# A batched fp32 matmul with 1 MiB loads and stores: a small early DMA from an input into the output, and stores six batches behind the loads

## Chip, cores, metric

One core of one Trainium2 chip. The metric is the device time of one execution in microseconds (us), lower is better. The profile's span is about 2.0 us shorter than this time (125.2 against 127.17 us).

## The reference

```
a: (16, 512, 512) float32      # batch, k, m
b: (16, 512, 512) float32      # batch, k, n
out = np.matmul(a.transpose(0, 2, 1), b)      # (16, 512, 512) float32
```

Each batch reads 2 MiB and writes 1 MiB: 50.33 MB in all.

## The kernel before

One queue, SyncE's, issues all loads and stores, 1 MiB each: 128 partitions with 8192 contiguous bytes each. VectorE casts a and b to bf16, TensorE multiplies, ScalarE copies PSUM to an output tile. The store of batch i comes in the queue behind the load of batch i + LAG.

```python
LAG = 4
NL = LAG + 1          # load buffers
NB = 2                # bf16 buffers
NO = LAG + 2          # output buffers
...
def load(i):
    j = i % NL
    if i >= NL:
        nc.sync.wait_ge(s_acast, i - NL + 2)
    nc.sync.dma_start(a_ts[j][:], a_v[i]).then_inc(s_a[j], 16)
    nc.sync.dma_start(b_ts[j][:], b_v[i]).then_inc(s_b[j], 16)

def store(i):
    nc.sync.wait_ge(s_ev1, i + 1)
    nc.sync.dma_start(out_v[i], o_ts[i % NO][:]).then_inc(s_o[i % NO], 16)

for i in range(LAG):
    load(i)
for i in range(batch):
    if i + LAG < batch:
        load(i + LAG)
    store(i)
for j in range(NO):
    nc.sync.wait_ge(s_o[j], 16 * len(range(j, batch, NO)))
...                   # VectorE casts, TensorE matmuls (16 of 128x512 per batch)
for i in range(batch):
    if i >= NO:
        nc.scalar.wait_ge(s_o[i % NO], 16 * (i // NO))
    for h in range(H):
        nc.scalar.wait_ge(s_mm, H * i + h + 1)
        nc.scalar.copy(
            out=o_ts[i % NO][:, 2 * h:2 * h + 2, :], in_=ps_ts[(i % NB) * H + h][:]
        ).then_inc(s_ev1 if h else s_ev0, 1)
```

Of the kernel before, what the change touches and what calls it, by code (L numbers as in the profile page):

```python
# [1 line left out]

# [4 lines left out]

@with_exitstack
def kernel(
    ctx: ExitStack,  # L10
    tc: tile.TileContext,
    a: bass.AP,
    b: bass.AP,
    out: bass.AP,
):
    nc = tc.nc
    P = 128
    batch, K, M = a.shape
    _, _, N = b.shape
    KO = K // P  # L20
    MO = M // P
    f32 = mybir.dt.float32
    bf = mybir.dt.bfloat16



    a_v = a.rearrange("bat (ki ko) m -> bat ki ko m", ko=KO)
    b_v = b.rearrange("bat (ki ko) n -> bat ki ko n", ko=KO)
    out_v = out.rearrange("bat (mi mo) n -> bat mi mo n", mo=MO)

    LAG = 4
    NL = LAG + 1
    NB = 2
    NO = LAG + 2
    H = MO // 2

    pool = ctx.enter_context(tc.tile_pool(name="sb", bufs=1))
    psum = ctx.enter_context(tc.tile_pool(name="ps", bufs=1, space=bass.MemoryType.PSUM))
    a_ts = [pool.tile([P, KO, M], f32, name=f"a{j}") for j in range(NL)]
    b_ts = [pool.tile([P, KO, N], f32, name=f"b{j}") for j in range(NL)]  # L40
    abf_ts = [pool.tile([P, KO, M], bf, name=f"abf{j}") for j in range(NB)]
    bbf_ts = [pool.tile([P, KO, N], bf, name=f"bbf{j}") for j in range(NB)]
    o_ts = [pool.tile([P, MO, N], f32, name=f"o{j}") for j in range(NO)]
    ps_ts = [psum.tile([P, 2, N], f32, name=f"ps{j}") for j in range(NB * H)]

    s_a = [tc.alloc_semaphore(f"s_a{j}") for j in range(NL)]
    s_b = [tc.alloc_semaphore(f"s_b{j}") for j in range(NL)]
    s_o = [tc.alloc_semaphore(f"s_o{j}") for j in range(NO)]
    s_acast = tc.alloc_semaphore("s_acast")
    s_bcast = tc.alloc_semaphore("s_bcast")  # L50
    s_mm = tc.alloc_semaphore("s_mm")
    s_ev0 = tc.alloc_semaphore("s_ev0")
    s_ev1 = tc.alloc_semaphore("s_ev1")

    with tc.tile_critical(no_gpsimd_drain=True):  # L55
# [6 lines that stand above are left out]
            nc.sync.dma_start(b_ts[j][:], b_v[i]).then_inc(s_b[j], 16)  # L62

        def store(i):
            nc.sync.wait_ge(s_ev1, i + 1)
            nc.sync.dma_start(out_v[i], o_ts[i % NO][:]).then_inc(s_o[i % NO], 16)

# [10 lines that stand above are left out]
            n = 16 * (i // NL + 1)  # L78
            if i >= NB:
                nc.vector.wait_ge(s_mm, H * (i - NB + 1))  # L80
            nc.vector.wait_ge(s_a[i % NL], n)
            nc.vector.tensor_copy(out=abf_ts[i % NB][:], in_=a_ts[i % NL][:]).then_inc(s_acast, 1)  # L82
            nc.vector.wait_ge(s_b[i % NL], n)
            nc.vector.tensor_copy(out=bbf_ts[i % NB][:], in_=b_ts[i % NL][:]).then_inc(s_bcast, 1)  # L84

        nc.tensor.sem_inc(s_ev0, 1)
        with nc.tensor.Fori(0, batch // NB):
            for u in range(NB):
                a_m = abf_ts[u][:].rearrange("p ko (mi mo) -> p ko mo mi", mo=MO)
                nc.tensor.wait_ge(s_bcast, 1).then_inc(s_bcast, -1)  # L90


                nc.tensor.wait_ge(s_ev0, 1).then_inc(s_ev0, -1)  # L93
                for mo in range(MO):
                    for ko in range(KO):
                        mm = nc.tensor.matmul(  # L96
                            ps_ts[u * H + mo // 2][:, mo % 2, :],
                            a_m[:, ko, mo, :],
                            bbf_ts[u][:, ko, :],
                            start=(ko == 0),  # L100
                            stop=(ko == KO - 1),
                        )
                    if mo % 2:
                        mm.then_inc(s_mm, 1)

        for i in range(batch):
            if i >= NO:
                nc.scalar.wait_ge(s_o[i % NO], 16 * (i // NO))
# [7 lines that stand above are left out]
# [1 line left out]
_INS = ['a', 'b']  # L117
_OUTS = [((16, 512, 512), 'float32')]


# [23 lines left out]
```

## Time and profile before

| | before |
|---|---|
| time, median of 3 | 126.56 us (126.44 to 126.85) |
| the profiled execution | 127.17 us, span 125.2 us |
| DMA queue | 96.6% of 16 engines' span |
| TensorE, VectorE, ScalarE busy | 59%, 31%, 27% |

From the page: the span, the rows of the granted TensorE clock, of the DMA engines' busy share and of their rate in 40 equal slices (3.1 us each), and the line of the one DMA queue (packets, MB, share of 16 engines).

```profile
span 125.2 us, 757 instructions
...
PEclk9999999999997786999558997786999558997785
DMA  3999999999999999999999999999999999999971
GB/s 81 422 422 427 429 422 427 422 348 432 387 419 416 429 429 401 419 429 440 424 424 419 432 437 422 424 419 435 437 419 422 422 432 432 424 424 424 416 317 81
...
q1 hardware_dynamic: 6912, 50.33, 96.6%
```

The DMA engines hardly ever rest: the kernel is bound by them. Two slices stand out, 348 near 26 us, and 317 near the end.

The view by windows puts numbers on these. Its columns: stretch, its length, then busy time and instruction count of PE, PEld, DVE, ACT and POOL, the granted clock, the DMA engines' busy share, and GB/s.

```profile
core 0: us, PE busy (x) PEld busy (x) DVE busy (x) ACT busy (x) POOL busy (x), PEclk, DMA share, GB/s
14.00:26.00 12.00, 10.49 (x46) 4.96 (x45) 5.66 (x6) 5.39 (x6) 0.00 (x0) 1.00 1.02 425
26.00:28.00 2.00, 2.00 (x11) 0.91 (x9) 0.84 (x1) 1.01 (x1) 0.00 (x0) 1.00 0.99 311
...
60.00:90.00 30.00, 20.33 (x64) 7.91 (x64) 10.33 (x9) 8.11 (x8) 0.00 (x0) 0.78 1.01 427
118.00:119.00 1.00, 0.22 (x2) 0.00 (x0) 0.00 (x0) 0.74 (x1) 0.00 (x0) 1.00 0.80 336
119.00:120.00 1.00, 0.00 (x0) 0.00 (x0) 0.00 (x0) 0.27 (x1) 0.00 (x0) 1.00 0.37 156
120.00:121.00 1.00, 0.00 (x0) 0.00 (x0) 0.00 (x0) 0.00 (x0) 0.00 (x0) 1.00 0.94 393
121.00:122.00 1.00, 0.00 (x0) 0.00 (x0) 0.00 (x0) 0.00 (x0) 0.00 (x0) 0.50 1.00 410
122.00:123.00 1.00, 0.00 (x0) 0.00 (x0) 0.00 (x0) 0.00 (x0) 0.00 (x0) 0.50 0.66 270
```

From 26 to 28 us the engines are busy (0.99) and yet move 311 instead of 425 GB/s: their packets take longer. From 119 to 120 us they are not busy (0.37): they have nothing to do. The second case is the "hole".

The chain of waits (start, length, what) shows what the hole waits for: batch 15's matmuls and its last copy.

```profile
112.87 0.04 issue
112.92 5.32 PE ps L96 x16
118.24 0.02 issue
118.26 1.01 ACT o L111
```

The last store is issued when that copy is done, in the timeline (start, length, engine, instruction):

```profile
118.26 1.01 ACT L111 COPY o<-ps 128x1024 f32<-128x1024 f32 x1 [1.85 <-PE ps L96]
119.30 0.33 SPq L66 DMA_DIRECT2D out_dram<-o  x1
```

### The profile page before, as it was taken

To read this page: it belongs to the slowest core of one execution; us is meant where nothing else is said; L and a number is where in the kernel's file an instruction comes from. 1 tells how busy PE (TensorE), PEld (TensorE's weight loads), DVE (VectorE), ACT (ScalarE), POOL (GpSimd) and SP (SyncE) were. 2 spreads that over 40 slices of the span, in tenths; PEclk is the share of its full clock that TensorE was granted. 3 is DMA by queue.
4 is the path that set the end of the run, shared out by engine and by line. 5 is a ranking of instruction groups with operands and counts; after the bars stand their busy time and mean duration, and the time that the engine had idled before them with its cause. 6 is when DMAs were issued, how large, how long until landed. Compare 5 with 4: busy or idle time off the path is not lost. (4 is left out here: it accounts for less than half of the span.)

```text
span 125.2 us, 757 instructions
## 1 busy us (share of the span) xinstructions
PE 74.0 (59%) x256; PEld 30.5 (24%) x256; DVE 39.3 (31%) x32; ACT 33.7 (27%) x33; POOL 0.2 (0%) x4
## 2 busy tenths in 40 slices
PE   0009999593708829473495916939391697809700
PEld 0003354242303203141132503313150232304200
DVE  0153365333060330613324052332505233160000
ACT  4000364533510421515024330331433033421410
POOL 0000000000000000000000000000000000000000
PEclk9999999999997786999558997786999558997785
DMA  3999999999999999999999999999999999999971
GB/s 81 422 422 427 429 422 427 422 348 432 387 419 416 429 429 401 419 429 440 424 424 419 432 437 422 424 419 435 437 419 422 422 432 432 424 424 424 416 317 81
DMA packets 6912, 50.33 MB, mean 402 GB/s; under 512 B 768, under 2 KB 768, under 8 KB 768
## 3 DMA queue, kind: packets, MB, share of 16 engines
q1 hardware_dynamic: 6912, 50.33, 96.6%
HBM read 33.55 MB, written 16.78 MB: 402 GB/s over the span
## 5 line engine op out<-in xcount | busy, mean ns | idle before, releaser
L96 PE MATMUL ps<-bbf,abf 128*128 128x512 bf16 x256 | 74.0, 455 | 44.2 <-PEq L93 44.2
L111 ACT COPY o<-ps 128x1024 f32<-128x1024 f32 x32 | 32.4, 1013 | 84.7 <-PE ps L96 84.7
L96 PEld LDWEIGHTS ps<-bbf,abf 128*128 128x128 bf16 x256 | 30.5, 124 | 87.2 <-issue 72.3
L82 DVE CAST abf<-a 128x2048 bf16<-128x2048 f32 x16 | 19.6, 1227 | 54.3 <-DMA a<-in_a_dram 52.6
L84 DVE CAST bbf<-b 128x2048 bf16<-128x2048 f32 x16 | 19.6, 1227 | 19.1 <-DMA b<-in_b_dram 19.1
L111 ACT ACT_TABLE_LOAD x1 | 1.3, 1283 | 0.9 <-SPq L55 0.9
L128 POOL MEMSET const-bfloat16-1.0<- 128x1 bf16 x1 | 0.1, 101 | 0.0
L128 POOL MEMSET const-uint8-127<- 128x1 uint8 x1 | 0.1, 101 | 0.0
L128 POOL MEMSET const-float32-0.0<- 128x1 f32 x1 | 0.1, 98 | 0.2 <-issue 0.2
L128 POOL MEMSET const-float32-1.0<- 128x1 f32 x1 | 0.1, 98 | 0.0
## 6 DMA issues: line engine op xcount, KB each, us to landing
a<-in_a_dram SPq DMA_DIRECT2D x16, 1024.0 KB, 25.3
b<-in_b_dram SPq DMA_DIRECT2D x16, 1024.0 KB, 26.0
out_dram<-o SPq DMA_DIRECT2D x16, 1024.0 KB, 23.7
```

The lines of the kernel that those rows point to most:

```text
L82: nc.vector.tensor_copy(out=abf_ts[i % NB][:], in_=a_ts[i % NL][:]).then_inc(s_acast, 1)
L84: nc.vector.tensor_copy(out=bbf_ts[i % NB][:], in_=b_ts[i % NL][:]).then_inc(s_bcast, 1)
L96: mm = nc.tensor.matmul(ps_ts[u * H + mo // 2][:, mo % 2, :], a_m[:, ko, mo, :], bbf_ts[u][:, ko, :], start=(ko == 0), stop=(ko == KO - 1),)
L111: nc.scalar.copy(out=o_ts[i % NO][:, 2 * h:2 * h + 2, :], in_=ps_ts[(i % NB) * H + h][:]).then_inc(s_ev1 if h else s_ev0, 1)
L128: nc = _bacc.Bacc("TRN2", target_bir_lowering=False, num_devices=1)
```

## The change

Two things. The stores come six batches behind the loads, with eight output buffers and still five load buffers, so that the last inputs arrive earlier and batch 15 is computed while stores are still queued. And a small DMA, issued from ScalarE at the start, copies one run of 512 B for each of 16 stretches of each batch from a into out (256 runs), which the stores overwrite later; the first store waits for it. The intent can only be guessed from the code: to pay whatever the first write to the output costs while the first load is on its way.

```diff
-    LAG = 4
-    NL = LAG + 1
+    LAG = 6
+    NL = 5
...
+    s_w = tc.alloc_semaphore("s_w")
...
         def store(i):
+            if i == 0:
+                nc.sync.wait_ge(s_w, 16)
             nc.sync.wait_ge(s_ev1, i + 1)
...
+        E = 16
+        first = out.rearrange("bat (e r) n -> e bat r n", e=E)[:, :, 0, 0:P]
+        nc.scalar.dma_start(
+            first, a.rearrange("bat (e r) m -> e bat r m", e=E)[:, :, 0, 0:P]
+        ).then_inc(s_w, 16)
         for i in range(batch):
             if i >= NO:
```

## The prediction

> **What bounds the kernel now.** The DMA engines: the page's third part gives their queue 96.6% of the span (125.2 us, 50.33 MB); TensorE is busy 59%, VectorE 31%, ScalarE 27%. The view by windows shows 425 to 428 GB/s in undisturbed stretches (14 to 26, 60 to 118 us). Rate is lost in three places:
>
> 1. Start: the first 8 packets of the first load (8192 B each) took 1.04 to 1.16 us; the usual packet takes 309 ns. Little moves before 2.6 us.
> 2. The first stores. The windows give 311 GB/s from 26 to 28 us (first store) and 388 from 32 to 35 us (second). In the trace's packet records, 34 packets of the first store's stretch are over 100 ns above normal (mostly 0.5 to 0.64 us), then 12, 5 and 6 at the second to fourth stores (up to 1.07 us), hardly any later. The excess is 0.54 + 0.28 + 0.14 + 0.17 = 1.1 us per engine. It looks like a one-time cost of first writing to the output.
> 3. The tail. The chain of waits ends in batch 15's matmuls and copy (112.9 to 119.3 us); only then is the last store issued, and the queue runs dry: 118 to 123 us moves 313 GB/s, 119 to 120 only 156. Those bytes at 427 GB/s would end about 0.9 us earlier.
>
> **What the change does.** No arithmetic changes.
> (a) Stores come six batches behind, with eight output buffers. Batch 15's load is followed by seven stores instead of five (program order), so the last inputs land about two stores (4.9 us at 2.46 us per MB) earlier, and the last copy ends near 115 us while stores are queued until about 121. Item 3 should vanish: -0.9 us. Load buffers stay five and loads wait for casts as before, so some 20 us of work stays queued; I expect no starving. TensorE gets a batch every 4.9 us for longer; a throttled batch took up to 6.4 us, but this is not critical.
> (b) The small DMA (256 runs of 512 B, 16 per engine) touches the output during the start, when the engines wait for first packets anyway. If it pays item 2 in advance, the first stores run at about 425 GB/s: I take 80%, -0.9 us. It is issued from ScalarE, [...]: its 0.13 MB cost 0.3 us at 427 GB/s, and slow first packets add to that, partly hidden in the start: +0.5 us. The issue on ScalarE is off the chain (its first copy starts at 13.3 us); the new wait before store 0 is met long before 17 us.
>
> Sum: 126.56 - 0.9 - 0.9 + 0.5 = 125.3 us, all on the critical path, since the DMA engines are. At most about 2 us (1.6%) are to be had.
>
> **Predicted** 125.3 us, 124.4 to 126.3 eight times in ten. Faster by over 2%: 0.05; within 2%: 0.92; slower by over 2%: 0.03.
>
> **What would show it.** Right: no slice near 348 GB/s at the first store (now near 37 us), few packets over 0.5 us there, slow packets in the first 5 us instead; no hole in the DMA row before the last store, and batch 15's copy ending well before it; a span near 124 us. The tail alone right: hole gone, slow store packets still there, some 125.9 us.
>
> **What would make it wrong.** The small runs, 1 MB apart, may be slow in memory and hold the engines for some us at the start; the one-time cost may belong to each stretch of the output, so that 512 B do not pay it; or the loads' wait for casts may leave the queue short.

(One clause is cut where marked: the ground given for the small DMA taking time of the same 16 engines. At that point this was an assumption; the trace of the changed kernel shows it (16.4 packets under way at a time with it, 16.2 without; see "Why the prediction was wrong"). The sum: 126.56 - 0.9 - 0.9 + 0.5 = 125.26, so 125.3 us. The 80% and the +0.5 us are estimates of mine, the latter from 0.13 MB at 427 GB/s and the first packets of 1.04 to 1.16 us. The doubts about small runs in memory and about a cost for each stretch of the output are guesses; in the changed kernel 252 of the 256 small runs took 27 ns.)

## The result, and the profile after

Ratios in this document are the mean time of one kernel's fast runs over that of the other's in the same rounds, so not quite the ratio of the medians beside them.

| | before | after |
|---|---|---|
| time, median of 4 | 126.59 us (126.44 to 126.85) | 126.91 us (126.54 to 126.93) |
| ratio to before | | 1.0017 (0.9992 to 1.0041) |
| span of the profiled execution | 125.2 us | 124.9 us |

The change does nothing measurable. Every local sign of it is there, though. The page of the changed kernel, the same rows, with the line of the small DMA's queue and of its issue (count, KB, us from issue to landing):

```profile
span 124.9 us, 758 instructions
...
PEclk9999999999999995589977999599999976859555
DMA  2999999999999999999999999999999999999991
GB/s 60 412 428 435 425 425 422 420 420 420 422 407 399 393 428 435 422 425 414 428 422 425 425 430 433 422 430 420 430 433 425 422 425 430 428 430 425 428 386 50
...
q1 hardware_dynamic: 6912, 50.33, 96.5%
q10 hardware_dynamic: 272, 0.13, 0.4%
...
out_dram<-in_a_dram ACTq DMA_DIRECT2D x1, 128.0 KB, 5.7
```

The windows that answer to those of before, with the same columns; the stretch in front of the first store is now at 36 to 38 us:

```profile
36.00:38.00 2.00, 2.00 (x11) 1.05 (x10) 1.23 (x1) 0.92 (x1) 0.00 (x0) 1.00 1.02 352
...
60.00:90.00 30.00, 17.47 (x64) 7.46 (x64) 10.29 (x9) 8.12 (x9) 0.00 (x0) 0.89 1.01 427
118.00:119.00 1.00, 0.00 (x0) 0.00 (x0) 0.00 (x0) 0.00 (x0) 0.00 (x0) 0.50 1.01 426
119.00:120.00 1.00, 0.00 (x0) 0.00 (x0) 0.00 (x0) 0.00 (x0) 0.00 (x0) 0.50 1.01 426
120.00:121.00 1.00, 0.00 (x0) 0.00 (x0) 0.00 (x0) 0.00 (x0) 0.00 (x0) 0.50 1.06 451
121.00:122.00 1.00, 0.00 (x0) 0.00 (x0) 0.00 (x0) 0.00 (x0) 0.00 (x0) 0.50 0.60 254
122.00:123.00 1.00, 0.00 (x0) 0.00 (x0) 0.00 (x0) 0.00 (x0) 0.00 (x0) 0.50 0.24 98
```

And the chain of waits, which ends 5 us earlier than before and no longer reaches the end of the kernel:

```profile
107.86 0.04 issue
107.90 5.32 PE ps L99 x16
113.22 0.02 issue
113.24 1.01 ACT o L121
```

The hole before the last store is gone: 426 and 451 GB/s from 118 to 121 us. But the rate now falls after it, 254 and 98 GB/s from 121 to 123 us. Taken over 118 to 123 us, the five rates average 313 GB/s before and 331 after. The idle time has moved from in front of the last store to behind it. That is the whole riddle in five lines.

The trace's packet records resolve it. Each engine ends its share of a DMA with a packet of 4 B, which raises the semaphore (the trace before has 768 of them, 16 for each of 48 DMAs, and as many semaphore updates). The 16 such packets of one store say when each of the 16 engines was done with it. For the last two stores (us from the span's start, sorted, computed from the packet records):

```
                      store of batch 14              store of batch 15
                      first    last      first    median   mean     last     last - last
before                118.54   120.764   122.65   122.72   122.75   123.217   2.453
after                 118.68   120.645   121.13   122.16   122.03   123.098   2.453
```

Before, 15 of the 16 engines finish within 0.24 us of each other, at 122.65 to 122.89, and one at 123.22. After, they finish anywhere between 121.13 and 123.10. The mean came 0.72 us earlier, close to the 0.9 us predicted for the hole; the last came 0.12 us earlier. And in both, the engine that is last with batch 15 ends exactly 2.453 us after the last one with batch 14, which is 8 packets at the undisturbed spacing of 306 ns. So the last engine did not wait in the hole at all. The hole belonged to engines that were ahead of it. The kernel waits until all 16 engines are done with a store, so it ends with the last one.

The stretch in front of the first store is still slow, too: 352 GB/s from 36 to 38 us. In the packet records, 22 packets of 8192 B there are more than 100 ns over the normal 309 ns (34 before). The trace doesn't name engines, but a packet can be linked to the next one of its engine, which starts about where it ends (309 ns long at a spacing of 306; two engines in step can be taken for each other). The links show that the slow packets belong to the load in front of the store, not to the store itself. Before, all 34 started between 25.7 and 27.5 us, and no engine was done with that load, and so none could begin the store behind it, until 27.6 us. In that run, the slow packets started before the trace has any packet that writes the output. So the trace that the prediction was made from already spoke against "a one-time cost of first writing to the output".

### The profile page after: what moved, and what is told of

It reads as the page before. It is cut to its first block, busy times and chain, and to the rows that moved or that the text cites. A ratio compares the mean times of both kernels' runs of the same rounds, so it can differ in the third digit from the quotient of the medians.

```text
span 124.9 us, 758 instructions
## 1 busy us (share of the span) xinstructions
PE 69.6 (56%) x256; PEld 29.9 (24%) x256; DVE 39.3 (31%) x32; ACT 33.7 (27%) x33; POOL 0.2 (0%) x4
## 3 DMA queue, kind: packets, MB, share of 16 engines
q1 hardware_dynamic: 6912, 50.33, 96.5%
## 5 line engine op out<-in xcount | busy, mean ns | idle before, releaser
L99 PE MATMUL ps<-bbf,abf 128*128 128x512 bf16 x256 | 69.6, 435 | 43.6 <-PEq L96 43.6
L99 PEld LDWEIGHTS ps<-bbf,abf 128*128 128x128 bf16 x256 | 29.9, 121 | 82.9 <-issue 65.6
```

The costliest lines, as they stand in the source:

```text
L99: mm = nc.tensor.matmul(ps_ts[u * H + mo // 2][:, mo % 2, :], a_m[:, ko, mo, :], bbf_ts[u][:, ko, :], start=(ko == 0), stop=(ko == KO - 1),)
```

## The experiments

Two theories were on trial for the time. **S**: the slowest engine sets it, and idle time of the others is worth little. **T**: the sum of the prediction holds, and the small DMA costs much more than thought. For the slow packets near the first store: **F**, a cost of the first write to the output, which an early write pays; **P**, engines in step that get in each other's way.

The table has what the packet records say in each profiled execution. "Excess" is the time of 8192 B packets above 309 ns, summed and divided by 16 engines, in us; "slow" packets are over 100 ns above 309.

```
                 slow near      excess           last store's completions
                 first store    <12 us  >12 us   first    mean     last     ratio to before (95%)
before           34             0.44    1.41     122.65   122.75   123.22
before_again     42             0.50    1.31     122.16   122.33   122.74
after            22             0.44    1.07     121.13   122.03   123.10   1.0017 (0.9992-1.0041)
after_again       9             0.67    1.09     121.28   121.95   123.07   1.0026 (1.0003-1.0048)
lag_only         17             0.35    1.26     120.96   121.77   122.75   0.9965 (0.9921-1.0009)
lag_only_2        5             1.12    1.10     121.17   122.11   123.07   0.9968 (0.9931-1.0004)
touch_only       21             0.40    0.96     121.28   122.10   123.13   1.0015 (0.9966-1.0064)
touch_only_2     27             0.61    1.07     122.97   123.07   123.52   1.0004 (0.9969-1.0039)
touch_sbuf        0             0.95    1.07     121.83   122.73   124.06   1.0055 (1.0011-1.0099)
touch_rows        0             0.70    0.88     121.67   122.50   123.72   1.0019 (0.9975-1.0062)
```

### 1. Each part alone

The later stores alone: the changed kernel without the small DMA and its wait.

```diff
-            if i == 0:
-                nc.sync.wait_ge(s_w, 16)
...
-        E = 16
-        first = out.rearrange(...)
-        nc.scalar.dma_start(first, a.rearrange(...)).then_inc(s_w, 16)
```

> The changed kernel without the small DMA: only the stores six batches behind. Theory S (slowest engine): in the kernel before, the hole at the end belongs to engines that were early; the one engine that ended last (its last store's completion 0.33 us after the next) had no hole, so six batches behind can give at most some 0.3 us, and the time is 126.2 to 126.7 us, with some 30 or more packets over 0.5 us still near the first store. Rival T (sum): the hole cost 0.9 us and the small DMA took it back, so this alone gives 125.5 to 125.9 us.

> The run with only the later stores once more, as the base for the two runs with extra bytes on this chip and for a second interval: theory S expects 0.996 to 1.000 of before, as in the first (0.9965); theory T 0.993.

Measured: 126.70 us against 126.96 (0.9965), and 126.47 against 126.79 (0.9968). Both intervals reach just over 1; pooled by their widths (an estimate of mine from the two) they give 0.9967 with about 0.0028 either side, so some 0.4 us. The medians differ by less, 0.26 and 0.32 us. The 0.9 us of theory T would be 0.993. In the profile the last stretch looks as in the changed kernel:

```profile
118.00:119.00 1.00, 0.00 (x0) 0.00 (x0) 0.00 (x0) 0.00 (x0) 0.00 (x0) 0.50 0.99 418
...
121.00:122.00 1.00, 0.00 (x0) 0.00 (x0) 0.00 (x0) 0.00 (x0) 0.00 (x0) 0.50 0.52 221
122.00:123.00 1.00, 0.00 (x0) 0.00 (x0) 0.00 (x0) 0.00 (x0) 0.00 (x0) 0.50 0.14 57
```

The expectation of 30 slow packets near the first store failed: there were 17, and 5 in the second execution, with no small DMA at all.

The small DMA alone: the changed kernel with four batches again.

```diff
-    LAG = 6
+    LAG = 4
```

> The changed kernel with the stores four batches behind again: only the small DMA. Theory S: the small DMA's 16 runs cost each engine 0.4 to 0.5 us near 5 us, and spare the slow engines about as much at the first stores, so the time is within 0.4 us of before, 126.3 to 126.9 us. Rival T: the small DMA costs more than it gives by about the 0.9 us that the hole would have given, so 127.3 to 127.8 us.

> The run with only the small DMA once more (first 1.0015, interval 0.9966 to 1.0064). Expected 1.000 to 1.004: the small DMA takes 0.4 us of each engine near 5 us and gives back about as much. If it were worth the 0.9 us predicted less 0.5 us of cost, 0.997.

Measured: 127.23 us against 126.96 (1.0015) and 127.05 against 126.79 (1.0004). By itself it is worth nothing, within 0.5%. Theory T needed 127.3 to 127.8 us; the first median lies just below that range, the second clearly below, and the ratios speak for S. The slow packets near the first store are hardly fewer than before (21 and 27 against 34 and 42).

This profile shows another thing: at four batches behind, there was no hole in the first execution. Its chain of waits:

```profile
112.78 3.63 PE ps L99 x16
116.41 0.02 issue
116.44 1.01 ACT o L121
```

Batch 15's matmuls took 3.63 us here, at a granted clock of 1.00, against 5.32 us in the profile before, at a mean granted clock of 0.68. The last copy ended at 117.45 instead of 119.27 us, before the queue ran dry.

### 2. The kernels themselves, once more

> The kernel before, unchanged, for a second profiled execution. In the first one batch 15's matmuls ran at half clock (5.31 us) and the last store was issued at 119.3 us, with a hole; in the run with only the small DMA they ran at full clock (3.63 us), the last copy ended at 117.5 us, and there was no hole, at the same four batches. If the hole hangs on the clock in that execution, it comes and goes here with the length of batch 15's matmuls, while the span stays 124.5 to 125.2 us. If it is a fixed part of the kernel, it is here whatever the clock. Near the first store some 30 slow packets in either case.

> The changed kernel, unchanged, on the same chip as the others of this call, for a like-for-like time. Expected within 0.4 us of before by every theory; its last packets again spread over more than 1 us between engines, with no hole.

The kernel before, unchanged, took 126.70 us with a span of 124.7 us, 0.5 us shorter than in its first profile. Batch 15's matmuls were slowed again (5.30 us in the chain of waits, mean granted clock 0.68; "half clock" in the expectation is too strong, as only some 3.4 us of them were at half), and there was a hole, but a shallower one: 320 GB/s from 119 to 120 us instead of 156, since the copy ended at 118.78 us. So the hole's depth changes from execution to execution, and the first profile had caught a deep one. Its last engine again did not wait: 120.284 us with batch 14, 122.737 with batch 15, the same 2.453 us. The changed kernel took 127.06 us against 126.84 (1.0026, interval above 1): if anything, slower.

### 3. Is the small DMA paying for a first write?

The same 256 reads, but landing in SBUF, so that nothing writes the output early:

```diff
+    w_t = pool.tile([16, batch, P], f32, name="w")
...
-            first, a.rearrange("bat (e r) m -> e bat r m", e=E)[:, :, 0, 0:P]
+            w_t[:], a.rearrange("bat (e r) m -> e bat r m", e=E)[:, :, 0, 0:P]
```

> The changed kernel with the same 256 reads of 512 B from a, but landing in SBUF: no early write to the output. If the slow packets near the first store are a first-write cost of the output that the small DMA pays in part (theory F), they are back at 30 or more over 0.48 us-class packets near the first store (34 before, 17 after) and the time is 0.3 to 0.6 us above the changed kernel, 127.2 to 127.5. If instead the small DMA only shifts the engines against each other (theory P, lockstep), the count stays near 17 and the time near 126.9.

(The expectation mixes two thresholds: before has 34 packets over 0.41 us, and the changed kernel 22 over 0.41 us, as in the table, of which 17 are over 0.48 us.)

Measured: 127.89 us (1.0055), and **no** slow packet near the first store. Its windows there, and at its small DMA:

```profile
36.00:38.00 2.00, 1.80 (x9) 1.00 (x10) 0.77 (x1) 0.00 (x0) 0.00 (x0) 1.00 1.03 430
5.00:10.00 5.00, 0.00 (x0) 0.00 (x0) 1.45 (x2) 0.00 (x0) 0.00 (x0) 1.00 1.01 378
```

430 GB/s at the first store without any early write, where the changed kernel with its early write has 352. Theory F is refuted: the slow packets are not a first-write cost. One execution alone would be thin evidence for a count that varies this much, but lag_only_2 had only 5 without an early write, touch_only had 21 and 27 with one, and all of the 34 and 42 in the kernel before started before its first store. The time is longer all the same. The small runs into 16 partitions took up to 0.73 us each (252 of 256 took 27 ns in the changed kernel), which shows as 378 GB/s from 5 to 10 us, and slow packets came later instead: the excess after 12 us is 1.07 us, the same as in the changed kernel (1.07 and 1.09).

Small stores with exactly the partitions of the real ones, for batches 0 to 3:

```diff
...
+        nc.gpsimd.memset(w_t[:], 0.0).then_inc(s_z, 1)
+        nc.scalar.wait_ge(s_z, 1)
+        for i in range(4):
+            nc.scalar.dma_start(out_v[i][:, 0, 0:P], w_t[:]).then_inc(s_w, 16)
```

> The changed kernel with the small DMA replaced by four small stores from SBUF, 128 rows of 512 B each, with the same partitions [...] as the stores of batches 0 to 3: 32 runs per engine. Theory F with a cost that belongs to engine and place: fewer than 5 packets over 0.48 us near the first store, the extra runs cost 0.4 us more per engine, and the time is 126.2 to 126.7 us. If the cost belongs to something a small write does not pay, the slow packets stay (15 to 35) and the time is 127.2 to 127.6 us.

(Cut where marked: that equal partitions mean equal engines. That was my assumption; the trace doesn't name engines.)

Measured: 127.50 us (1.0019); no slow packet near the first store, as F would have it, but with the run above this is no support for F. The time expected with it (126.2 to 126.7 us) did not come. Slow packets after 12 us still sum to 0.88 us per engine, now mostly after 55 us.

### 4. Shifting work between engines

If the slowest engines set the time, work moved from late to early engines should help. The base is the later stores alone, where in the first profiled execution eight engines ended at 120.96 to 121.48 us and eight at 122.18 to 122.75 (the expectation below gives them some 0.7 us too low). The second execution, profiled later, has no such two groups: its engines ended spread from 121.17 to 123.07. The plan was to give eight engines more bytes by DMAs of 8 runs. In number the records bear this out: the pages of the two split kernels have 800 packets under 512 B, 32 more than the 768 before, so 8 and not 16 closing packets for each of the four small DMAs; and in low8_extra below, eight engines have 388 packets of 8192 B and eight have 384, so four such DMAs went to the same eight. "Lowest-numbered" in the expectations is my name for these eight; the trace doesn't name engines, so that was not shown, and which eight are early was a guess. Where the expectations stated it as a fact, it is cut as marked, and with it, from that of balance_early, that the loaded eight would be four runs (4 x 306 ns = 1.2 us, an estimate from that spacing) behind the others from 20 us on, and from that of low8_extra, that the split last store pointed to the loaded eight as the early ones.

```diff
             # balance_late: the last store, after stores six batches behind
...
+                for p, q in [(0, 96)] + [(r, r + 8) for r in range(96, P, 8)]:
+                    nc.sync.dma_start(out_v[i][p:q], o_ts[i % NO][p:q]).then_inc(s_o[i % NO], 16)
             # balance_early: the same split of the load of a, batch 3
```

> Stores six batches behind, no small DMA, and the last store (batch 15) split: 96 partitions on all 16 engines (6 runs each) and four pieces of 8 partitions, [...] so these 8 engines get 10 runs of 8192 B and the others 6 instead of 8. In the run with only the later stores, eight engines ended at 120.3 to 120.8 us and eight at 121.5 to 122.0. Theory S (the slowest engine sets the time): if the early eight are the lowest-numbered, the end comes about 0.5 to 0.6 us earlier than with even shares (two runs less, 0.6 us), near 126.0 to 126.3; if they are the others, it comes 0.6 us later, 127.2 to 127.5. Rival T (a shared limit): the total is the same, so 126.7 as in that run.

> The same split, but of one early load (a of batch 3) instead of the last store. Each engine's total is as in the run with the split last store, so theory S expects the same shift of the time by 0.5 to 0.6 us, in the same direction. [...] if slow packets near the first store come from engines in step (theory P), there are fewer than the 17 of over 0.41 us seen in the run with only the later stores; if not, as many.

Measured: 126.72 us (0.9989, 0.9969 to 1.0009) for the split last store, between the three outcomes expected, so inconclusive. Its packet records say why. The eight engines with the four extra pieces ended at 121.65 to 122.92 us, the other eight at 121.55 to 122.16. With even shares, two runs (0.61 us) more for the other eight and two less for the loaded ones, the other eight would have ended last, at 122.16 to 122.78 (an estimate from these ends). So in this execution the loaded eight were the early ones, but six of their single-run pieces were slow (0.58 to 1.31 us), which ate up what the shift could give. And 131.09 us (1.0338) for the split load, which none of the theories foresaw. Its windows show where:

```profile
12.00:16.00 4.00, 4.00 (x16) 1.86 (x15) 1.41 (x3) 1.55 (x2) 0.00 (x0) 1.00 1.01 428
16.00:19.00 3.00, 2.88 (x14) 1.27 (x12) 1.15 (x1) 1.57 (x3) 0.00 (x0) 1.00 1.06 352
19.00:22.00 3.00, 1.41 (x7) 0.82 (x8) 1.23 (x1) 0.93 (x1) 0.00 (x0) 1.00 1.08 202
22.00:25.00 3.00, 2.21 (x11) 0.91 (x9) 0.00 (x0) 1.77 (x2) 0.00 (x0) 1.00 0.98 131
```

From 19 to 25 us the engines are busy all the time and move 131 to 202 GB/s; 175 packets there are slow. What both split runs have in common is small DMAs of 8 neighbouring partitions, 0.26 MB in all; six of the pieces of balance_late were slow as well. low8_extra below moves as many bytes in DMAs of 8 runs with partitions four apart, and takes 127.19 us. But no run here varied the partitions alone, so the cause is not shown. The times of these two runs say nothing about S or T.

Then extra bytes without such pieces: 0.26 MB of useless loads, either on eight engines (partitions four apart) or on all sixteen.

```diff
             # in load(i), after b
+            if i == 3:                                                   # low8_extra
+                for r in range(4):
+                    nc.sync.dma_start(w_t[r:32:4], a_v[0][r:32:4]).then_inc(s_w, 16)
+            if i == 3:                                                   # all16_extra
+                nc.sync.dma_start(w_t[:, 0, :], a_v[0][:, 0, :]).then_inc(s_w, 16)
```

> Only the later stores (no small DMA), plus four extra loads of 8 runs of 8192 B into an unused tile, after the load of batch 3: [...] so these engines get 4 runs (1.2 us) more and the other 8 none. In the run with only the later stores eight engines ended a good 1 us before the others[...]. Theory S (the slowest engine sets the time): the extra 0.26 MB cost nothing or nearly so, the time stays within 0.3 us of the run with only the later stores, and the eight early engines now end about 1.2 us later. Rival T (the total of bytes at the common rate sets it): 0.26 MB / 427 GB/s = 0.6 us more.

> The control: the same extra 0.26 MB at the same place, but spread over all 16 engines (128 runs of 2048 B, 8 for each engine). Both theories expect 0.6 to 0.7 us more than the run with only the later stores, because the slow engines get their share as well. If this costs 0.6 us and the other nothing, the time is set by the slow engines and not by the bytes.

Measured with the base (0.9968): 127.19 us (1.0014) on eight engines, 127.78 us (1.0059) on sixteen. So 0.46% and 0.91% over the base, about 0.6 and 1.2 us; from the six times of each run, with noise of 0.38 and 0.33 us either side (95%, computed from them). The expectation that the eight would be free failed; 0.6 us is what T said for them. But T said 0.6 us for the sixteen as well, and they cost about twice that, outside the noise, so a bare count of bytes at a common rate doesn't fit either. Linking each packet to the next one of its engine in the packet records separates the engines:

```
low8_extra, packets of 8192 B per engine: last store's completion, us
8 engines with 388 packets:  122.40 122.71 122.79 122.87 122.88 122.89 122.90 123.23
8 engines with 384 packets:  121.22 121.23 121.24 121.27 121.27 121.29 121.30 121.44
```

The loaded engines end last again, with the eight others done 1.8 us before the end. S needs this, but it doesn't prove S: for the time of this run T's 0.6 us was nearer than S's 0.3 us at most. What failed is my guess that the loaded eight had 1 us to spare. Whether they were the late ones to begin with, or being behind brings slow packets with it, is open.

### 5. Do engines in step make the slow packets?

By then theory P had a correlation for it: in the two executions of the kernel before, the 16 engines completed the load of a just in front of the first store within 258 and 266 ns (34 and 42 slow packets), and in the executions with 0 to 5 slow packets within 620 to 890 ns (with an exception: low8_extra, 1351 ns in two clusters, 29 slow packets). So the engines were spread on purpose in the kernel before, with graded small loads into an unused tile; the control gives every engine the same number. The plan was that one engine gets up to 15 runs of 1024 B more than another; at 306 ns for 8192 B a run is 38 ns, so up to 0.6 us between the engines (an estimate from that spacing). That a load of k runs goes to k engines, always the same ones first, is an assumption taken from the loads of 8 runs in low8_extra (388 packets against 384); for these two kernels it was not counted, and what stated it engine by engine is cut from the first expectation as marked.

```diff
...
+        for k in range(15, 0, -1):                                       # stagger4
+            nc.scalar.dma_start(w_t[0:4 * k:4, k - 1, :], b_v[0][0:4 * k:4, 0, 0:256]).then_inc(s_w, 16)
+        for k in range(8):                                               # even4
+            nc.scalar.dma_start(w_t[0:64:4, k, :], b_v[0][0:64:4, 0, 0:256]).then_inc(s_w, 16)
```

> The kernel before (stores four batches behind, no early write of the output), plus 15 small loads at the start on ScalarE's queue, on 15, 14, ... 1 of the engines, one run of 1024 B each, into an unused tile: [...]. Theory P (the slow packets near the first store come from engines that run in step): the completions of one load before the first store spread over more than 500 ns (261 ns in both executions of the kernel before), and fewer than 12 packets near the first store are over 100 ns above normal (34 and 42 before). If the slow packets belong to the first writing of the output, which nothing does early here, 30 to 45 as before. The time within 0.5 us of before in either case.

> The control: the kernel before plus 8 small loads at the start on ScalarE's queue, each one run of 1024 B on every one of the 16 engines, so that all get the same (8 runs, about the mean of the staggered kernel). Theory P: the spread stays under 400 ns and 20 or more packets near the first store are over 100 ns above normal. If any additional DMA at the start removes the slow packets, there are fewer than 12 here too.

Measured: the staggered kernel had a spread of 1736 ns and 22 slow packets near the first store (127.88 us, 1.0089, 1.0052 to 1.0126). The control had a spread of 367 ns and none (128.35 us, 1.0100, 1.0058 to 1.0143). Theory P as stated failed both ways: many slow packets with engines apart, none with engines in step. Each count is of one execution, though, and such counts swing (17 and 5, 22 and 9), so this is a strong sign and not proof. The staggered kernel also took 1.1 us more than before, where 0.5 us had been allowed. What makes the slow packets stays open. Known is that they come and go between executions of one kernel, that the profiled executions with three unlike small DMAs at the start (touch_sbuf, touch_rows, even4) had none near the first store, with or without a write to the output, and that none of these kernels was faster.

The control has a second lesson. There the last engine was done with batch 14 at 121.45 us and with batch 15 at 124.51, 3.06 us later instead of 2.453, and all 16 ended between 124.37 and 124.51. In that execution everybody waited for the last store's issue, which started at 121.02 us because batch 15's matmuls took 6.40 us at a mean granted clock of 0.56. So the hole can be what sets the time, at four batches behind, when batch 15 comes late enough.

## Why the prediction was wrong

- **DMA engines bind the kernel: right.** 96.6% before and 96.5% after; the rate in undisturbed stretches is 427 GB/s in both. The DMA issued from ScalarE took time of the same engines: from 5.00 to 6.25 us, 5.7 packets of the small DMA and 10.7 of the loads were under way at a time on average, 16.4 together, and from 6.25 to 7.00 us 16.2 of the loads alone. Its runs stand in the gaps between the loads' packets.
- **"Item 3 should vanish: -0.9 us." The hole vanished, most of the gain did not come.** Batch 15's last copy ended at 114.25 us (about 115 predicted), and no rate was lost before the last store. Alone, this part gave about 0.4 us (0.9965 and 0.9968). The step that failed is "all on the critical path, since the DMA engines are": a rate summed over 16 engines was read as time of the last one. The mean completion of the last store did come 0.72 us earlier, the last completion 0.12 us, since the last engine never waited in the hole. Besides, the profile that the 0.9 us was read from was an execution 0.6 us slower than the median, with a deeper hole than the next one (156 against 320 GB/s).
- **"If it pays item 2 in advance ... I take 80%, -0.9 us": this is the term that failed most.** The step that failed is the mechanism of item 2: slow packets of the load in front of the first store were taken for a one-time cost of first writing the output, though all 34 started before the first store did. With the same reads and no write to the output there was not one of them near the first store; with the small DMA alone there were still 21 and 27. At four batches the excess after 12 us went from 1.41 and 1.31 us per engine to 0.96 and 1.07, some 0.35 us less; at six batches from 1.26 and 1.10 to 1.07 and 1.09, some 0.1 us. Not 0.9.
- **"+0.5 us" for its cost: about right in size, as time of each engine.** 16 runs of 27 ns are 0.43 us on each engine; no run measured this cost alone. But "partly hidden in the start" was wrong. The first run of 512 B began at 5.0 us, when the first engine had moved its 8 packets and the completion of the first load (it ended at 5.004 us; the next three ended at 5.028 to 5.050 us, and the runs that started in each step of some 24 ns rose from one to three and then four), and the DMA landed 5.7 us after its issue. That runs wait for the end of a load is no rule, though: in touch_sbuf the small DMA's runs began at 1.95 us, before the first load was through, and in touch_rows 306 of the 512 runs were followed at once by a packet of the loads' queue, clearly by another run only 55 (matched by time; the rest is ambiguous). How an engine chooses between two queues is not shown.
- **The sum.** Predicted: -0.9 - 0.9 + 0.5 = -1.3 us. Measured: +0.17% and +0.26%, or +0.2 to +0.3 us. The parts alone add up to about -0.3% + 0.1%. The remaining 0.4% is as large as the intervals; one reading is that with four batches the small DMA's cost falls on engines that wait in the hole anyway. That is argued, not shown.
- **The starving feared for the five load buffers did not come**: the page gives 412 to 435 GB/s in every slice except those near the first store and at both ends.

A version that may beat both by a little: the later stores without the small DMA, 0.3% under the kernel before in two calls (each interval reaches just over 1) and 0.5 to 0.6% under the changed kernel by the ratios of different calls. None of these differences reaches 1%.

## What to carry to other kernels

When DMA engines bind a kernel, look at when each of the 16 is done with the last transfer before pricing a dip in the summed rate: idle time of engines that are ahead can be free, as it was here (without the hole the mean completion came 0.72 us earlier, the last 0.12 us), and removing it then only moves it behind their last packet. (even4 is the exception here: there the last engine waited too, 3.06 us between its last two completions instead of 2.453.) Check first whether the slow packets come before or after the event that is blamed for them. Test a supposed first-touch cost with a control that makes the same traffic without the touch, because slow packets come and go between executions of one and the same kernel (17 and 5, 22 and 9). And compare the profiled execution's time with the median: a feature read from one slow execution may be noise in part (the hole: 156 GB/s in one, 320 in the next).

## What the records show besides

- The engines of one DMA finish apart. With equal bytes on all 16, the last store's completions lay 2.0 us apart in the changed kernel (121.13 to 123.10 us), and 2.2 us in touch_sbuf (121.83 to 124.06).
- Single packets are slow in an otherwise steady stream. 8192 B packets, normally 309 ns, took 0.41 to 1.43 us after the first 12 us, nearly all in loads (before: 34 in the load in front of the first store, 25 in later loads), for a sum of 0.7 to 1.4 us per engine after the first 12 us in all kernels but the split load (5.3 us). What causes them is open.
- The runs of 512 B from HBM to HBM came about 23.6 ns apart on an engine, 21.7 GB/s (512 B / 23.6 ns), where 8192 B packets come 306 ns apart, 26.8 GB/s.
- The engines did not start alike: the first packet of the first load took 1.04 to 1.16 us on eight engines before, and up to 1.34 us in the changed kernel, while the other eight engines before started 0.6 us later and took 0.31 to 0.39 us.
- The hole at the end went with the granted TensorE clock of the execution: at four batches behind, batch 15's 16 matmuls took 3.63 us at a granted clock of 1.00 (touch_only, no hole) and 5.32 us at 0.68 (before, with the hole), and the last copy ended at 117.45 and 119.27 us, 1.8 us apart.
